# Two-layer hybrid backbone block: norm statistics, stage loads and context products in another program order

## The chip, the cores and the metric

The kernel runs on one core of one Trainium2 chip. The metric is the device time of one execution in microseconds (us); the kernel before has a median of 3649.86 us in 3 runs (3645.42 to 3652.5). TensorE (PE) multiplies, VectorE (DVE), ScalarE (ACT) and GpSimd (POOL) do elementwise work, and SyncE (SP) issues the DMAs.

## What is computed

Two layers over 1024 latent tokens and 256 context tokens, width 1024. In each layer a modulated RMS norm feeds one input projection, whose columns go to three mixers (neighbourhood attention, differential attention, a bidirectional SSD with a convolution over its `xbc` columns). Their outputs go through an output projection and a gated residual. A second modulated norm feeds a gated MLP with a convolution on its gate, again with a gated residual. The last layer needs no context output.

```python
h = rms_norm(x, g_mix[l]) * (1.0 + sc1) + sh1
hc = rms_norm(ctx, g_mix[l]) * (1.0 + csc1) + csh1
y, yc = token_mixers(h, hc, ...)
x = x + g1 * (y @ w_out[l])
h = rms_norm(x, g_ffn[l]) * (1.0 + sc2) + sh2
x = x + g2 * conv_glu(h, w_up[l], conv_w[l], conv_b[l], w_dn[l])
# if ctx_out: the same for ctx with c_ctx's modulation
```

## The kernel before

Activations lie transposed, 128 features by tokens, in three token chunks: 0 and 1 (512 tokens each) and 2 (the 256 context tokens). Float32 operands are split into a high and a low part by an ACT cast and a subtraction on DVE or POOL, and a product is three matmuls: high by high, high by low, low by high (`mm3`, L1214 to L1216; `proj_chunk`, L423 to L425).

The kernel is written in a tile framework: the order of the instructions on each engine, SP's among them, is planned when it is built. A list scheduler takes of the ready instructions the one that stands first in the program (`prio` shifts that) by modelled times. On the chip each engine then runs its list in that order. A tile waits for what lay in its memory before. Pools are stacks on the left or on the right of SBUF.

**The norm.** `norm_sq` squares on ACT and adds up on DVE (L376). `norm_scale` multiplies the sum by a matrix of ones (L382) and makes the reciprocal root on ACT and DVE (L411, L415). `norm_apply` scales (L397), modulates (ACT, L93), and splits into `h_0`, `h_1`, `h_2` for the three chunks (L402, L403). In the second norm `ffn_norm` is a generator whose first step is `norm_scale`; its rest makes the operands B11 to B22 and T1 to T4 of a Winograd-like scheme of seven products (L1592 to L1626).

**Output projection** (`outproj`). The last pass ends in chunk 1's norm sum. `up_prologue` then makes the first products of the up projection from chunk 0, and `up_weights` splits the first pair's weights (`T42` and `T43` are their slots); after that the norm generator is run to its end.

**Down projection** (`ffn_down`). `x1d` holds the residual stream, `hdd` the seven operands, `hcd` the context's. Layer 0 runs three groups of 3, 4 and 4 k-tiles, each with a context part (24 matmuls of 256 columns a step, with tiles `hc`) and seven products; layer 1 runs one group of 11 without context. `product` loops over the k-tiles: a `br` load from `hdd` (L1510, 2 buffers in layer 1, 3 in layer 0), `fetch(1)` of a weight tile `wd` (L1475, 18 buffers in layer 1, 10 in layer 0), casts and splits to `bH`, `bL`, `wH`, `wL` (L1220, L1223), and 12 matmuls into four PSUM banks A or B. The order is B11 (A), T2 (B), B21 (A), T3, T4 (B), T1, B22 (A). `w_s2` makes T2's weight on DVE in two steps (L1532, L1534). `to` evicts a bank into `xt` (L1438); the `xt` loads (`load_x`, L1481) stand in the program behind T2. In layer 0's last group the context norm for layer 1 (`norm_next(2)`) stands behind T2's evictions; its matmul takes a bank of tag B, and T2's four stay in use until T4 is done.

**Hand-over.** At the end of layer 0's down stage three weight tiles `w_pre` for layer 1's `xbc` columns are loaded and split. After the stage pool `dn0` is closed, `h1b` is opened on the right and `norm_apply` runs for chunk 1. Then `mixer(1)` opens `m1_1` on the left, with three `pad` tiles whose edges POOL sets to zero (L540). `proj_many` runs the products of `w_pre` in the order context, chunk 0, chunk 1, into three banks `mm`; ACT copies each result into `pad` (L548).

## Time and profile before

| | |
|---|---|
| median of 3 runs | 3649.86 us (3645.42 to 3652.5) |
| the profiled execution | 3640.75 us, span 3639.0 us |
| TensorE busy | 3292.2 us, 90% of the span, 17970 matmuls |
| DVE, ACT, POOL busy | 65%, 42%, 48% |
| mean granted TensorE clock | 0.962 of full speed |
| DMA | 491.24 MB, mean 135 GB/s |

All rows are of that one execution; times in a row are counted from the span's start. Layer 0's output projection ends at about 1060, its down stage runs from about 1664 to 1994, the hand-over lies at 1990 to 2060, layer 1's output projection ends at about 2890 and its down stage runs from about 3389 to the end. A granted clock of 1.00 is 2.4 GHz and 0.50 is 1.2 GHz. Busy time of overlapped matmuls is modelled, so PE's pace is read from the spacing of its instructions. A release in brackets is inferred from semaphore events.

### The profile page before, as it was taken

How to read it: one execution, taken by the hardware profiler on the slowest of the kernel's cores; microseconds unless marked ns; L12 is line 12 of the kernel's file. 1: busy time of each engine (PE TensorE's matmuls, PEld its weight loads, DVE VectorE, ACT ScalarE, POOL GpSimd, SP SyncE). 2: the span in 40 equal slices, each digit the busy share in tenths (PEclk: the TensorE clock that was granted, in tenths of full speed). 3: DMA queues.
4: the chain of work that ended last, by engine and by line, in shares of the span. 5: the costliest groups of instructions: out<-in, count | busy, mean ns of one | idle time of the engine just before them, and what ended most of it. 6: DMA issues, size and time to landing. Idle time of an engine off the chain costs nothing. (4 is left out here: it accounts for less than half of the span.)

```text
span 3639.0 us, 50284 instructions
## 1 busy us (share of the span) xinstructions
PE 3292.2 (90%) x17970; PEld 2590.3 (71%) x17970; DVE 2348.0 (65%) x4208; ACT 1514.2 (42%) x2641; POOL 1743.8 (48%) x1319
## 2 busy tenths in 40 slices
PE   7998898889998999998998798998888979999799
PEld 3876676666777887887787676776666757777587
DVE  6635875778376555556867554885784566667653
ACT  4232434677253333323335333344674533333243
POOL 2136563656233444444554126763664455555344
PEclk8999999999899999999999899998999989999899
DMA  8255444753721222226334136347555422222633
GB/s 292 99 198 164 128 128 133 187 152 102 254 93 67 87 93 68 87 92 213 118 117 138 46 127 208 124 131 184 168 150 198 156 70 91 101 96 88 225 107 119
DMA packets 328473, 491.24 MB, mean 135 GB/s; under 512 B 28320, under 2 KB 182048, under 8 KB 327968
## 3 DMA queue, kind: packets, MB, share of 16 engines
q1 hardware_dynamic: 328224, 488.03, 42.0%
q8 instruction: 142, 2.33, 0.3%
q14 instruction: 107, 0.88, 0.1%
HBM read 349.25 MB, written 138.67 MB: 134 GB/s over the span
## 5 line engine op out<-in xcount | busy, mean ns | idle before, releaser
L269 POOL TENSOR_TENSOR wL<-wr,wH 128x1024 fp32r<-128x1024 f32 x80 | 203.5, 2547 | 418.9 <-ACT wH L268 385.5
L1223 POOL TENSOR_TENSOR wL<-wr,wH 128x1024 fp32r<-128x1024 f32 (+1 forms) x102 | 211.1, 2072 | 336.5 <-ACT wH L1220 310.8
L1223 POOL TENSOR_TENSOR wL<-wd,wH 128x512 fp32r<-128x512 f32 (+1 forms) x134 | 211.3, 1594 | 229.7 <-ACT wH L1220 222.8
L1223 POOL TENSOR_TENSOR wL<-ws,wH 128x512 fp32r<-128x512 f32 x168 | 253.9, 1531 | 127.9 <-ACT wH L1220 127.7
L754 DVE TENSOR_SCALAR_CACHE_REDUCE e<-s 128x512 f32<-128x512 f32 (+1 forms) x400 | 228.3, 588 | 94.7 <-PE s L753 91.3
L1223 DVE TENSOR_TENSOR bL<-br,bH 128x512 fp32r<-128x512 f32 x154 | 146.4, 955 | 153.9 <-ACT bH L1220 153.5
L93 ACT ACTIVATE e<-e,nm 128x1280 f32<-128x1280 f32 (+1 forms) x144 | 183.0, 1271 | 55.9 <-DVE nm L757 52.5
L1220 ACT CAST wH<-ws 128x512 fp32r<-128x512 f32 x168 | 98.0, 619 | 236.5 <-PE mm L1215 111.2
L1220 ACT CAST wH<-wr 128x1024 fp32r<-128x1024 f32 (+1 forms) x102 | 91.7, 905 | 251.2 <-PE mm L1215 189.8
L753 PE MATMUL s<-ks,qst 128*128 128x512 f32 (+1 forms) x400 | 162.7, 443 | 36.6 <-DVE e L754 23.3
L772 POOL TENSOR_TENSOR e<-e 128x1280 f32<-128x1280 f32 (+1 forms) x72 | 192.6, 2675 | 3.9
L770 POOL TENSOR_SCALAR e<-e,rho 128x1280 f32<-128x1280 f32 (+1 forms) x72 | 89.3, 1240 | 188.8 <-DVE rho L762 80.2
L1369 DVE SCALAR_TENSOR_TENSOR fa<-fpad,vc,fa 128x1282 f32<-128x1282 f32 (+1 forms) x88 | 140.5, 1652 | 36.6 <-ACT fa L93 36.6
L992 POOL TENSOR_SCALAR mf<-cs,lah 128x128 fp32r<-128x128 f32 x288 | 139.8, 501 | 48.0 <-PE s L994 46.3
L1220 ACT CAST wH<-wd 128x512 fp32r<-128x512 f32 (+1 forms) x134 | 86.7, 683 | 166.4 <-PE B L1215 88.1
L423 PE MATMUL mm<-h_0H,wH 128*128 128x512 f32 x320 | 135.6, 425 | 21.2 <-ACT pad L548 15.1
L1220 ACT CAST bH<-br 128x512 fp32r<-128x512 f32 x154 | 95.5, 620 | 137.8 <-DMA br<-hdd 65.1
L1215 PE MATMUL A<-bL,wH 128*128 128x512 f32 x352 | 142.3, 404 | 7.3 <-DVE bL L1223 7.0
L1216 PE MATMUL A<-bH,wL 128*128 128x512 f32 x352 | 139.4, 400 | 0.0
L424 PE MATMUL mm<-h_0L,wH 128*128 128x512 f32 x320 | 131.9, 412 | 1.9 <-DVE h_0L L403 1.9
L423 PE MATMUL mm<-h_1H,wH 128*128 128x512 f32 x320 | 132.3, 414 | 1.5 <-ACT z L93 1.5
L753 PEld LDWEIGHTS s<-ks,qst 128*128 128x128 f32 x400 | 74.0, 198 | 81.5 <-DVE e L754 50.4
(871 smaller groups left out, 10835.8 us busy)
## 6 DMA issues: line engine op xcount, KB each, us to landing
wr<-in_w_up_dram SPq DMA_DIRECT2D x94, 512.0 KB
br<-hdd SPq DMA_DIRECT2D x154, 256.0 KB
wa<-in_w_ada_dram SPq DMA_DIRECT2D x56, 512.0 KB
wr<-in_w_in_dram SPq DMA_DIRECT2D x48, 512.0 KB
hdd<-c SPq DMA_DIRECT2D x88, 256.0 KB
wr<-in_w_ada_dram SPq DMA_DIRECT2D x40, 512.0 KB
wd<-in_w_dn_dram SPq DMA_DIRECT2D x38, 512.0 KB
hdd<-fa SPq DMA_DIRECT2D x66, 256.0 KB
```

What stands on the lines that cost most here:

```text
L93: ins = S.activation(**kw)
L269: (eng or G).tensor_tensor(out=wl, in0=wr, in1=wh.bitcast(F32), op=ALU.subtract)
L423: PE.matmul(ps[:, :n], wh[:, ks], r, start=(i == 0), stop=False)
L753: PE.matmul(s_, qst[b, qt][:, mi], ks[b][:, mi, k0 + c:k0 + c + n], start=True, stop=True)
L754: V.tensor_scalar(out=e[:, c:c + n], in0=s_, scalar1=1.0, scalar2=None, op0=ALU.mult, op1=ALU.max, accum_out=mx[:, ci:ci + 1])
L772: G.tensor_tensor(out=es[0][:, 0:nk], in0=es[0][:, 0:nk], in1=es[1][:, 0:nk], op=ALU.add)
L992: (V if hh % 2 else G).tensor_scalar(out=mf[:, hh], in0=C(mk), scalar1=lah[:, e, c, h:h + 1], scalar2=1.0, op0=ALU.mult, op1=ALU.mult)
L1215: PE.matmul(ps, wh, bl, start=False, stop=False, skip_group_check=True)
L1216: PE.matmul(ps, wl, bh, start=False, stop=last, skip_group_check=True)
L1220: S.copy(out=out_h, in_=src)
L1223: le.tensor_tensor(out=out_l, in0=src, in1=out_h.bitcast(F32), op=ALU.subtract)
L1369: V.scalar_tensor_tensor(out=a[:, :W], in0=pads[r][:, j:j + W], scalar=vcol(l, fw + j), in1=a[:, :W], op0=ALU.mult, op1=ALU.add)
```

## The change

Four things move in program order, and one pool moves in memory.

- In the down stage each weight tile and each `xt` tile is loaded by `fetch`, and each such load is tied behind the last operand load issued before it in the program (`lead`, a `br` or a context tile). It is an order on SP, without a semaphore. In layer 1 two such loads follow each `br`, the `xt` loads alternating with weights from the fifth weight on; in layer 0 two follow each context pair and three each `br`.
- In layer 0's last group the context norm for layer 1 stands ahead of B11, and chunk 0's `norm_scale` and half of chunk 1's squares ahead of B22.
- The context products of `w_pre` stand ahead of chunk 1's remaining squares and `norm_apply`; their copies into `pad` follow in the mixer.
- `m1_1` lies on the right instead of the left.
- In `outproj` the first step of the last norm generator (`norm_scale` of chunk 1) stands ahead of `up_prologue`.

```diff
-    def norm_apply(tmp, l, i, xt, ci, rs=None):
+    def norm_apply(tmp, l, i, xt, ci, rs=None, scaled=False):
...
-        scaled = rs is not None
-        if not scaled:
+        if rs is None:
             rs = norm_scale(tmp, ci)
...
-        with phase(f"m1_{l}") as p:
+        with phase(f"m1_{l}", "right" if l else "left") as p:
...
-            proj_many(w_pre, ALLC if l == 0 else [ALLC[2], ALLC[0], ALLC[1]], [xbc_ev(b) for b in range(nb)])
+            evs = [xbc_ev(b) for b in range(nb)]
+            for ev, ps in zip(evs, pre_ps):
+                with prio(-400):
+                    ev(ps, *ALLC[2])
+            proj_many(w_pre, MAINC if pre_ps else ALLC, evs)
+            pre_ps.clear()
...
+            lead = [None]
...
-                    todo = [(kt, h) for h in range(2) for kt in grp]
+                    pend = []
 
                     def fetch(n):
-                        for _ in range(min(n, len(todo))):
-                            kt, h = todo.pop(0)
+                        for _ in range(min(n, len(pend))):
+                            dst, src = pend.pop(0)()
+                            ins = SP.dma_start(out=dst, in_=src)
+                            if lead[0] is not None:
+                                tc.add_manual_dep(ins.ins, lead[0].ins.name, nosync, reason="order of loads")
+
+                    def load_raw_dn(kt, h):
+                        def go():
+                            raw[kt, h] = p.tile([128, 1024], F32, tag="wd", name="wd", bufs=10 if full else 18)
+                            return raw[kt, h], w_dn[l, (kt + h * NP) * 128:(kt + h * NP + 1) * 128, :]
+
+                        return go
+
+                    def load_xt(o, ci):
+                        c0, n = ALLC[ci]
+                        return lambda: (xt[o][:, c0:c0 + n], x1d[l][o, :, c0:c0 + n])
+
+                    xs = [load_xt(o, ci) for ci in ((2, 0, 1) if full else (0, 1)) for o in range(KT)] if gi == 0 else []
+                    for h in range(2):
+                        for kt in grp:
                             if pre_dn:
                                 raw[kt, h] = pre_dn.pop(0)
-                                continue
...
+                            else:
+                                pend.append(load_raw_dn(kt, h))
+                                if not full and len(pend) > 4 and xs:
+                                    pend.append(xs.pop(0))
+                    pend.extend(xs)
+                    fetch(2 if gi else 0)
...
-                    fetch(len(pre_dn) + 1)
...
+                    tail = fin and not last
+                    A = banks("A")
                     if full:
                         ps = banks("B")
...
-                                SP.dma_start(out=t.bitcast(F32), in_=hcd[l][kt + h * NP, e])
-                            fetch(1)
+                                lead[0] = SP.dma_start(out=t.bitcast(F32), in_=hcd[l][kt + h * NP, e])
+                            fetch(2)
...
-                        load_x(2)
...
+
+                    if tail:
+                        exp_tables()
+                        open_h(f"h{l + 1}")
+                        norm_next(2)
...
-                            SP.dma_start(out=br, in_=hdd[l][BN.index(nm), kt])
-                            fetch(1)
+                            lead[0] = SP.dma_start(out=br, in_=hdd[l][BN.index(nm), kt])
+                            fetch(3 if full else 2)
...
-                    load_x(0)
-                    load_x(1)
+                    fetch(len(pend))
                     to(A, [(1, 0), (1, 1), (0, 1)])
                     to(B, [(0, 1)])
-                    if tail:
-                        exp_tables()
-                        open_h(f"h{l + 1}")
-                        norm_next(2)
...
                     to(A, [(1, 1)], (1, 1))
+                    if tail:
+                        rs0 = norm_scale(tmp, 0)
+                        sq_next(1, range(4, 8))
                     product(A, "B22", w_s4, False, True)
                     if tail:
                         w_pre.extend(load_w(w_in[l + 1, B_XBC + b]) for b in range(3))
-                        sq_next(1, range(4, 8))
-                        norm_apply(tmp, l + 1, 0, xt, 0)
+                        norm_apply(tmp, l + 1, 0, xt, 0, rs0)
                     to(A, [(0, 1)], (0, 1))
             open_ps(mm=3)
             if not last:
+                c0, n = ALLC[2]
+                for wh, wl in w_pre:
+                    proj_chunk(wh, wl, c0, n, lambda ps, c0, n: pre_ps.append(ps))
                 open_h2(f"h{l + 1}b")
                 sq_next(1, range(0, 4))
                 norm_apply(tmp, l + 1, 0, xt, 1)
...
                 norms = [ffn_norm(l, tmp, xs[ci], ci, first) for ci in reversed(cis)]
+            next(norms[0])
             up_prologue(l, fx["n"])
```

## Rows read from the trace of the kernel before

**Rows 1.** The page, busy us (share of the span) x instructions of each engine.

```profile
PE 3292.2 (90%) x17970; PEld 2590.3 (71%) x17970; DVE 2348.0 (65%) x4208; ACT 1514.2 (42%) x2641; POOL 1743.8 (48%) x1319
```

**Rows 2.** Windows, layer 1's down stage: busy by engine, PEclk, DMA share, GB/s.

```profile
3420.00:3430.00 10.00, 4.24 (x10) 3.38 (x11) 4.79 (x8) 0.62 (x1) 0.00 (x0) 0.50 1.05 404
...
3470.00:3480.00 10.00, 10.00 (x46) 8.29 (x45) 4.46 (x4) 4.06 (x7) 4.28 (x3) 1.00 0.31 90
```

**Rows 3.** SP in time, both down stages: start, us issuing, line, what, count.

```profile
1677.78 2.79 SPq L1475 DMA_DIRECT2D wd<-in_w_dn_dram  x4
...
3401.14 0.33 SPq L1510 DMA_DIRECT2D br<-hdd  x1
3402.40 8.45 SPq L1475 DMA_DIRECT2D wd<-in_w_dn_dram  x9
...
3419.32 0.32 SPq L1510 DMA_DIRECT2D br<-hdd  x1
```

**Rows 4.** ACT in time, layer 1's down stage; brackets: idle before, its end.

```profile
3409.34 0.62 ACT L1220 CAST bH<-br 128x512 fp32r<-128x512 f32 x1 [5.07 <-DMA br<-hdd]
...
3425.09 0.62 ACT L1220 CAST bH<-br 128x512 fp32r<-128x512 f32 x1 [9.48 <-DMA br<-hdd]
```

**Rows 5.** PE in time, hand-over from layer 0's down stage to layer 1's mixer.

```profile
2003.83 0.28 PE L425 MATMUL mm<-h_2H,wL 128*128 128x256 f32 x1
...
2008.23 2.07 PE L382 MATMUL t<-acc,cs 128*128 128x512 f32 x2 [4.12 <-DVE acc L376]
...
2025.45 0.80 PE L423 MATMUL mm<-h_0H,wH 128*128 128x512 f32 x1 [15.14 <-ACT pad L548]
...
2045.16 0.40 PE L423 MATMUL mm<-h_1H,wH 128*128 128x512 f32 x1
```

**Rows 6.** POOL and DVE in time, the same hand-over.

```profile
2023.12 0.17 POOL L540 MEMSET pad<- 128x2 f32 x3 [1.69 <-DVE h_1L L403]
...
2023.60 2.50 DVE L403 TENSOR_TENSOR h_1L<-xt,h_1H 128x512 fp32r<-128x512 f32 x4 [0.53 <-ACT h_1H L402]
```

**Rows 7.** DVE and PE in time, end of layer 0's output projection.

```profile
1059.08 0.69 DVE L376 TENSOR_TENSOR acc<-acc,sq 128x512 f32<-128x512 f32 x1 [0.76 <-ACT sq L93]
...
1069.61 1.02 PE L382 MATMUL t<-acc,cs 128*128 128x512 f32 x2
...
1104.08 0.79 PE L1214 MATMUL mm<-T30H,wH 128*128 128x512 f32 x1 [3.77 <-DVE u L1329]
```

**Rows 8.** POOL and PE in time, end of layer 1's output projection.

```profile
2911.61 16.94 POOL L1223 TENSOR_TENSOR wL<-T42H,wH 128x512 fp32r<-128x512 f32 x1 [9.42 <-ACT wH L1220]
...
2928.61 0.80 PE L1216 MATMUL mm<-T10H,wL 128*128 128x512 f32 x1 [14.47 <-POOL wL L1223]
```

**Rows 9.** The chain that ended last: start us, us, what (layer 1's T2 products).

```profile
3465.16 0.91 PE B L1214 x4
...
3467.88 0.91 PE B L1214 x4
```

**Rows 10.** PE in time, waits in the down stages of both layers.

```profile
1682.57 1.19 PE L1214 MATMUL B<-hcH,wH 128*128 128x256 f32 x4 [6.46 <-DMA hcH<-hcd]
...
1919.08 0.80 PE L1215 MATMUL B<-bL,wH 128*128 128x512 f32 x1 [4.53 <-DVE bL L1223]
...
1973.52 0.72 PE L1215 MATMUL A<-bL,wH 128*128 128x512 f32 x1 [2.76 <-DVE bL L1223]
...
3393.12 1.73 PE L1214 MATMUL A<-bH,wH 128*128 128x512 f32 x4 [4.30 <-ACT bH L1220]
```

**Rows 11.** DVE in time, first eviction of B in layer 1's down stage.

```profile
3482.88 0.75 DVE L1438 SCALAR_TENSOR_TENSOR xt<-B,mods,xt 128x512 f32<-128x512 f32 x1 [1.53 <-PE B L1216]
```

**Rows 12.** Tiles xt and wd: line, operation, count, ns min/median/max, starts, forms.

```profile
L1438 DVE SCALAR_TENSOR_TENSOR xt<-A,mods,xt x96: 733/740/751, 1705.3 to 3635.2; 128x512 f32<-128x512 f32 x96
...
L1534 DVE TENSOR_TENSOR s<-wd x16: 683/692/2859, 1677.2 to 3423.7; 128x512 f32<-128x512 f32 x16
...
L1223 POOL TENSOR_TENSOR wL<-wd,wH x134: 1260/1302/2854, 1669.4 to 3621.9; 128x512 fp32r<-128x512 f32 x114, 128x1024 fp32r<-128x1024 f32 x20
```

More of the change, by code (lines that the diff above doesn't have):

```diff
@@ L1228, in hybrid_kernel @@
     pre_dn = []
+    pre_ps = []
     pre_wd = []
@@ L1471, in fetch @@
+                    xs = [load_xt(o, ci) for ci in ((2, 0, 1) if full else (0, 1)) for o in range(KT)] if gi == 0 else []
+                    for h in range(2):
+                        for kt in grp:
                             if pre_dn:
                                 raw[kt, h] = pre_dn.pop(0)
-                                continue
-                            raw[kt, h] = p.tile([128, 1024], F32, tag="wd", name="wd", bufs=10 if full else 18)
-                            SP.dma_start(out=raw[kt, h], in_=w_dn[l, (kt + h * NP) * 128:(kt + h * NP + 1) * 128, :])
@@ L1477, in load_x @@
-                    def load_x(ci):
-                        if gi == 0:
-                            c0, n = ALLC[ci]
-                            for o in range(KT):
-                                SP.dma_start(out=xt[o][:, c0:c0 + n], in_=x1d[l][o, :, c0:c0 + n])
-                    fetch(len(pre_dn) + 1)
+                            else:
+                                pend.append(load_raw_dn(kt, h))
+                                if not full and len(pend) > 4 and xs:
+                                    pend.append(xs.pop(0))
@@ L1545, in w_s4 @@
                         return t
-                    tail = fin and not last
-                    A = banks("A")
                     product(A, "B11", lambda kt: quarter(0, 0, kt), True, False)
@@ L1715, in hybrid_kernel @@
                     SP.dma_start(out=x0[k][:, c0:c0 + n], in_=xin[:, k, c0:c0 + n])
-        norm_apply(tmp, 0, 0, x0, 0, rs)
+        norm_apply(tmp, 0, 0, x0, 0, rs, True)
         for ci in range(1, 3):
```

## The prediction, made before the changed kernel was run

> **What bounds the kernel now.** I read the page first: TensorE is busy 90% of the span [rows 1], so only stretches in which it waits, or runs at the lower clock, can give time back. I then took 10 us windows over the places that the diff touches, and in them PE's timeline with what ended each idle gap. Three places lose much.
>
> First, the start of layer 1's down stage. Two windows show the contrast: PE busy 4.24 of 10 us at a granted clock of 0.50 (the 1.2 GHz level) with the DMA engines full at 404 GB/s, and later 10.00 of 10 us at clock 1.00 with 90 GB/s [rows 2]. SP's queue shows why: between the `br` issued at 3401.14 and the next one at 3419.32 stand nine `wd` weight loads (8.45 us of issuing, 0.94 each), then `xt` loads [rows 3]; the late `br` is cast only at 3425.09 [rows 4]. The bulk loads have free buffers from the start, `br` has two, so the planner let all bulk loads pass.
>
> Second, the hand-over from layer 0's down stage to layer 1's mixer: TensorE waits 4.12 us for the norm sum, then 15.14 us for the ACT copy into `pad` [rows 5]. That copy waits for `pad`'s memsets, and these for `h_1L` [rows 6]: on the left, `pad` lies where `xt` lay, and `xt` is read until the last norm step.
>
> Third, layer 0's output projection ends in a norm chain for which TensorE waits 3.77 us at its end [rows 7], and layer 1's in a wait of 14.47 us [rows 8].
>
> **Part 1, loads tied to their order (layer 1's down stage).** No work is added; the 18 `wd` and 16 `xt` loads go out two behind each `br`, instead of ahead. One step (12 matmuls) takes 2.72 us when nothing is missing [rows 9]. B11 and T2 have 11 steps each, 22 x 2.72 = 59.8 us; from the first product at 3393.12 [rows 10] to the first eviction of B at 3482.88 [rows 11] it is 89.8 us. The excess, 30.0 us, is the most that can come back. What is late next: (a) the two first steps move 0.26 + 1.05 MB, the loaded ones after them 0.26 + 0.79 MB; at 404 GB/s [rows 2] that is 3.2 and 2.6 us against 2.72: about 2 us lag in all. (b) DVE in T2: two weight differences and a low split, 3 x 0.69 [rows 12], 2.1 us in each step, and 12 evictions of A at 0.74 [rows 12], 8.9 us, before B21 may start: 31.7 us of DVE in 29.9. Before, the differences ran inside the stall. Group 2 of layer 0 has the same crowding in four steps, and TensorE waited 4.53 us there for `bL` [rows 10]. Eleven steps could cost 2.75 times that, 12.5 us, or the bare 2 us; I take 6, near the one stall that a row shows. Sum: 30.0 - 2 - 6 = **22 us saved**, ends 15 and 28. On SP, a `br` that waits for its buffer now holds back the loads queued behind it, but each of these is used four or more steps later (the `wd` of step 4 goes out behind the `br` of step 0), and that distance, 10.9 us, covers it.
>
> **Part 2, `pad` on the right, context products ahead of the second half's statistics.** `pad` and `cacc` (3 x 5152 + 2 x 5136 bytes, 25.1 KB per partition) now lie below `h1b` (32 KB), and both below `h1`. The stage pool `dn0` (66 KB by its buffers) ended under `h1` already, so the 57.1 KB below `h1` fall into `dn0`'s stretch and not into `xt`'s. `dn0`'s tiles are free when B22 ends, before any context product. Those were the first chunk before, too; they end at 2004.1 [rows 5]. Then come L382 (1.0 us at the higher clock [rows 7]) and 72 products on `h_0` at 2.72 / 12 us, 16.3 us: 2021.4. `h_1` was complete 15.8 us after the end of L382 (2010.30 to 2026.10 [rows 5, 6]), so now at 2020.9, in time. The first `h_1` product comes at 2021.4 instead of 2045.16 [rows 5], 23.8 us. This needs `h_0` by 2005; its statistics now run ahead of B22, and DVE is rid of the context norm there. GpSimd has three weight splits to do in the same stretch; a split held up by a DVE run took 16.94 us once [rows 8], and half of that in front of a context product would leave 15, the whole of it 7. I take **19 us**, ends 8 and 26 (the upper one if the 2.76 us wait in T1 and B22 [rows 10] goes too).
>
> **Part 3, layer 0's context norm ahead of B11 (group 2).** Nothing is added, and no DMA moves. 16 DVE steps of 256 columns, some 0.35 us each as half of a 512-column one [rows 12], 5.6 us, and as many on ACT move from the T1 and B22 products to B11 and T2, where DVE is already late by 4.53 us [rows 10]. T2's fourth PSUM bank waits for this norm's matmul, which B11's 10.9 us cover; without that cover it costs the norm's sum, within the same 8 us. Price 0 to 8, taken 4; given back in T1 and B22 0 to 2.76 [rows 10], taken 2. **2 us lost.**
>
> **Part 4, layer 0's group 0.** The weights of the next group, four of them issued at 1677.78 [rows 3], no longer go in front of the `hc` tile that TensorE waited 6.46 us for [rows 10]. But three early `br` now bring nine `xt`, 2.4 MB, 5.8 us at 404 GB/s, to the same place. **2 us saved**, ends -2 and 6.
>
> **Part 5, statistics ahead of the early products.** Layer 0: the last sum is done at 1059.77, its matmul ran at 1069.61 behind products, and TensorE's last wait for the chain ends at 1104.08 [rows 7]. Earlier by 9.8 us at best, 9 with the matmul's own time. But layer 1 shows what a DVE run without a gap does to GpSimd: a split that takes 1.30 us [rows 12] took 16.94 us, and TensorE waited 14.47 us for it [rows 8]. In layer 0 the splits of pair 0's weights lie next to the run, and moved forward the run meets the last of them, with TensorE's context rows behind. Between -4 and 9 us, **3 us saved**. Layer 1: the same held-up split ends the wait, so **nothing**, 0 to 3. The Trainium skill (SBUF — State Buffer, Who interferes with whom) says that a DVE instruction with two SBUF inputs and a GpSimd one that reads SBUF exclude each other for the whole of one instruction; by that rule alone a split would wait 0.7 us and layer 0 would give the 9 us. The row disagrees in size: 16.94 us is the run, not one instruction.
>
> **The sum.** 22 + 19 - 2 + 2 + 3 = 44 us. The profiled execution took 3640.75 us (span 3639.0), so 3597 by it; the median of the three runs, 3649.86, lies 9.1 us above, which gives **3606 us**. Between these places every stretch is shifted, not changed.
>
> **The rivals.**
> (A) DVE's earlier runs hold up GpSimd: layer 0's output projection loses 4 us instead of winning 3, part 2 gives 8, part 3 loses 8. For it: [rows 8]. Against: the median split takes 1.30 us beside DVE [rows 12]. 3606 + 7 + 11 + 6 = 3630 us.
> (B) The tied loads pace the stage: the loop of two `br` runs at 3.6 us for each of 17 loaded steps. 17 x 3.6 + 5 x 2.72 + 6 = 80.8 us, 9 saved instead of 22: 3619 us.
> (C) The change doesn't do what it says: `pad` still waits, or the planner puts the products where they were. Part 2 gives nothing: 3625 us. For it: the order of instructions is planned by modelled times, which no view shows.
> (D) Slower: in the loop of (B), `br` lands behind its tied loads each time. From 3401.14 to its cast at 3409.34 it took 8.2 us [rows 3, 4]; with three issues of 0.94 and 1.3 us of splits, 12.3 us for two steps, 6.15 for one. 17 x 6.15 + 5 x 2.72 + 6 = 124 us against 89.8: part 1 loses 34 and the whole is 3662 us. It decides from 5.5 us a step on. Against: at that pace the DMA engines would idle more than half of the time, and `br` would land sooner.
> (E) The new plan costs elsewhere what is won here: 3649 us.
>
> **How the numbers follow.** Forecast 50%, A 18%, B 11%, C 9%, D 5%, E 7%. The forecast's own range is 3586 to 3620, by the ends of parts 1 and 2 that can come together. With A, B and C the range is 3586 to 3634; D, E and part of the tails lie outside. A measurement of this kernel can tell 0.2%, 7 us. Faster by more: forecast, A, B, C, 88%; within it: E, 7%; slower: D, 5%.
>
> **What would show it.** Right: one `br` and two bulk loads alternate on SP after 3389 or its like; the granted clock stays at 1.00 from there; B's first eviction comes some 22 us sooner after the first A product; no idle time of TensorE is ended by `pad`; `h_1` products stand directly behind those on `h_0`. Wrong: GpSimd splits over 5 us in new places (A); products that wait for `bH` in every step (B, D); waits for `pad` (C); another length from the hand-over to layer 1's output projection (E).

## The result, and the profile after

The changed kernel took 3589.18 us (median of 4 runs, 3588.71 to 3605.27) against 3648.49 us (3645.42 to 3652.5, 4 runs) for the kernel before beside it: a ratio of 0.9848, 95% interval 0.9818 to 0.9877. It is 1.5% faster, inside the predicted range and 17 us below the predicted 3606. Its profiled execution has a span of 3587.6 us (3589.41 us in all), 51.4 us less than the span before.

The page has the engines' busy time, as [rows 1] did. The four engines have the same numbers of instructions, PE's share rises from 90% to 92%:

```profile
PE 3284.6 (92%) x17970; PEld 2582.9 (72%) x17970; DVE 2350.0 (66%) x4208; ACT 1515.8 (42%) x2641; POOL 1766.9 (49%) x1319
```

Layer 1's down stage, windows of 10 us (columns as in [rows 2]): the stretch at clock 0.50 with PE busy 4.24 is gone. The worst window now has 7.42 and a clock of 0.66, DMA still full; the later one is as in [rows 2].

```profile
3360.00:3370.00 10.00, 7.42 (x20) 5.63 (x20) 6.71 (x9) 3.22 (x6) 3.63 (x3) 0.66 1.03 378
3370.00:3380.00 10.00, 9.65 (x42) 7.96 (x43) 7.15 (x8) 3.30 (x6) 5.39 (x4) 1.00 1.04 412
...
3440.00:3450.00 10.00, 10.00 (x46) 8.29 (x45) 7.30 (x9) 4.15 (x7) 4.87 (x5) 1.00 0.36 102
```

SP's queue there, in time, answers to [rows 3]: one `br`, one `wd`, one `xt` in turn. In [rows 3] nine `wd` and six `xt` loads stood between two `br`.

```profile
3371.17 0.32 SPq L1535 DMA_DIRECT2D br<-hdd  x1
3371.53 0.43 SPq L1477 DMA_DIRECT2D wd<-in_w_dn_dram  x1
3372.01 0.43 SPq L1477 DMA_DIRECT2D xt<-x1d  x1
3373.57 0.32 SPq L1535 DMA_DIRECT2D br<-hdd  x1
```

The row of 8.45 us in [rows 3] is not issuing time, and my 0.94 us for one load was a wrong reading: the row merges nine issues and the gaps between them. Each took 0.33 us, and their starts lie 0.61 to 1.25 us apart; two of the nine, kernel before:

```profile
3404.89 0.33 SPq L1475 DMA_DIRECT2D wd<-in_w_dn_dram  x1
...
3406.14 0.33 SPq L1475 DMA_DIRECT2D wd<-in_w_dn_dram  x1
```

What SP waited for in the gaps no run shows. That the `br` stood behind the bulk loads does not hang on it.

The hand-over, PE in time, answers to [rows 5]: the waits of 4.12 and 15.14 us are gone but for 1.06 us at the norm's sum, `h_0` follows the sum at once, and `h_1` stands behind 17.2 us of products on `h_0`.

```profile
1996.94 1.13 PE L382 MATMUL t<-acc,cs 128*128 128x512 f32 x2 [1.06 <-DVE acc L376]
1997.51 0.80 PE L422 MATMUL mm<-h_0H,wH 128*128 128x512 f32 x1
...
2014.70 0.40 PE L422 MATMUL mm<-h_1H,wH 128*128 128x512 f32 x1
```

The end of the two output projections, POOL and PE in time, answers to [rows 7, 8]. In layer 0 there is now what only layer 1 had: one GpSimd split, of 1024 columns, lasts 20.61 us, and TensorE waits 17.41 us for it. Layer 1 has its wait of 14.47 us as before.

```profile
1075.07 20.61 POOL L1227 TENSOR_TENSOR wL<-wr,wH 128x1024 fp32r<-128x1024 f32 x1 [8.36 <-ACT wH L1224]
1095.73 0.58 PE L1220 MATMUL s<-c0H,wL 128*128 128x256 f32 x1 [17.41 <-POOL wL L1227]
1106.15 0.50 PE L1218 MATMUL mm<-T30H,wH 128*128 128x512 f32 x1 [0.78 <-DVE u L1334]
...
2875.97 16.94 POOL L1227 TENSOR_TENSOR wL<-T42H,wH 128x512 fp32r<-128x512 f32 x1 [9.42 <-ACT wH L1224]
2892.96 0.79 PE L1220 MATMUL mm<-T10H,wL 128*128 128x512 f32 x1 [14.47 <-POOL wL L1227]
```

To account for every microsecond I cut each span at the same events, read off PE's and DVE's timelines, and compare the pieces (us). No edit of the change stands in I, III, VI and VIII, though in VI the planned order came out different.

- I: start to the first norm sum (L382) of layer 0's output projection
- II: from there to the second set of T3 products of layer 0's up stage (norm, early products, first pair)
- III: to the last T3 of that stage
- IV: layer 0's down stage, to the first product on `h_2`
- V: the hand-over, to the first product of layer 1's dt weights
- VI: layer 1's mixer, to the first norm sum of its output projection
- VII: to the first T3 of layer 1's up stage
- VIII: to its last T3
- IX: to the first eviction of B in layer 1's down stage (B11 and T2)

From there to the end it is 156 us in all kernels.

| kernel | I | II | III | IV | V | VI | VII | VIII | IX |
|---|---|---|---|---|---|---|---|---|---|
| before | 1016.0 | 108.6 | 529.0 | 340.2 | 132.7 | 724.0 | 87.1 | 441.4 | 103.9 |
| changed | 1013.3 | 111.0 | 523.8 | 339.1 | 108.8 | 718.8 | 87.1 | 444.9 | 84.7 |
| changed, again | 1019.0 | 111.2 | 524.1 | 339.0 | 108.8 | 723.0 | 87.1 | 444.2 | 85.1 |
| statistics behind products | 1017.7 | 108.5 | 529.4 | 338.1 | 109.0 | 728.7 | 87.1 | 442.8 | 85.6 |
| pads left | 1016.2 | 110.9 | 527.1 | 339.2 | 126.7 | 727.0 | 87.1 | 443.6 | 85.6 |
| loads untied | 1015.2 | 110.4 | 526.8 | 341.8 | 108.8 | 728.8 | 87.1 | 444.8 | 106.3 |
| context norm late | 1015.1 | 111.2 | 526.7 | 337.9 | 121.1 | 735.1 | 87.6 | 441.9 | 85.5 |
| tied loads alone | 1014.4 | 107.8 | 530.1 | 329.8 | 134.6 | 721.2 | 87.1 | 443.4 | 86.4 |
| pair 0 on DVE | 1014.7 | 102.7 | 525.0 | 335.5 | 109.0 | 724.9 | 84.2 | 445.3 | 85.5 |
| the same, statistics behind | 1016.9 | 107.0 | 526.9 | 340.2 | 108.8 | 716.1 | 84.2 | 443.4 | 83.8 |
| fewer tied | 1016.9 | 111.3 | 526.5 | 336.7 | 108.8 | 716.1 | 87.1 | 443.4 | 88.0 |
| difference in B11 | 1022.4 | 111.4 | 524.0 | 338.7 | 108.8 | 719.9 | 87.1 | 444.1 | 86.2 |
| evictions spread | 1015.8 | 111.0 | 523.4 | 339.2 | 109.0 | 729.2 | 87.1 | 444.8 | 83.8 |
| pair 0 and evictions | 1012.1 | 102.6 | 526.0 | 341.5 | 108.8 | 735.9 | 84.7 | 443.2 | 84.1 |

Of the 51.4 us, 23.9 are in V, 19.2 in IX and 1.1 in IV; II gave 2.4 back. That makes 41.8 us where the edits are. The other 9.6 us are in I, III, VI and VIII. In the second execution of the same program (next section) the edited pieces give 41.3 us, and these four together are as long as before, within 0.2 us.

### The profile page after: what moved, and what is told of

Its sections match the earlier page's. It is cut to its first block, busy times and chain, and to the rows that moved or that the text cites. A ratio compares the mean times of both kernels' runs of the same rounds, so it can differ in the third digit from the quotient of the medians.

```text
span 3587.6 us, 50299 instructions
## 1 busy us (share of the span) xinstructions
PE 3284.6 (92%) x17970; PEld 2582.9 (72%) x17970; DVE 2350.0 (66%) x4208; ACT 1515.8 (42%) x2641; POOL 1766.9 (49%) x1319
## 5 line engine op out<-in xcount | busy, mean ns | idle before, releaser
L1227 POOL TENSOR_TENSOR wL<-wr,wH 128x1024 fp32r<-128x1024 f32 (+1 forms) x102 | 228.6, 2243 | 339.0 <-ACT wH L1224 304.4
L1219 PE MATMUL A<-bL,wH 128*128 128x512 f32 x352 | 141.7, 403 | 11.9 <-DVE bL L1227 11.7
```

Source lines behind the costliest of these rows:

```text
L1219: PE.matmul(ps, wh, bl, start=False, stop=False, skip_group_check=True)
L1227: le.tensor_tensor(out=out_l, in0=src, in1=out_h.bitcast(F32), op=ALU.subtract)
```

## The experiments

**The changed kernel once more.** How much of a difference between two profiles is the edit, and how much is any second execution?

> The changed kernel once more, unaltered, beside the other three on this chip. If the stretches that no edit touches (from the start to layer 0's output projection, 1013.3 us; from layer 1's first dt product to its output projection, 763.1 us; the two up stages, 523.8 and 444.9 us) differ between two executions of one program, they should move by up to 5 us here; if their lengths belong to the planned program, they should come back within 1 us and the differences of 5 to 10 us seen in the four kernels with one part undone are a new plan's. Total 3585 to 3600 us.

It took 3596.41 us, 0.986 of the kernel before beside it (0.9828 to 0.9892). Its profiled span is 3597.5 us, 9.9 us more than the first one's, from the same program: +5.6 in I, +4.2 in VI, and at most 0.8 in any other piece. II, IV, V, VII and IX agree within 0.4 us. So the 9.6 us that the first comparison has in untouched pieces are no effect of the change that I could show; the totals of one kernel scatter by 10 us and more (3585.35 to 3599.53 here). From here on I judge the pieces, and the totals only where they differ by more than that.

How far a piece can be trusted shows in the runs below that leave the order of PE's matmuls in it as in the changed kernel: II lies within 1.0 us there (110.4 to 111.4), V within 0.2 and VII at 87.1, but IX within 2.6 (83.8 to 86.4) and IV within 4.7 (335.5 to 340.2). In III all fourteen executions have one order on PE and take 523.4 to 530.1 us; nearly all of that lies in one of its twenty intervals, which takes 24.4 to 31.0 us.

**Each part undone.** Loads without the tie:

```
-  if lead[0] is not None:
+  if False:
       tc.add_manual_dep(ins.ins, lead[0].ins.name, nosync, reason="order of loads")
```

> The changed kernel without the ties between the loads: the list of loads and its alternation stay, only the order on SP is free. Theory (the tie is what counts, since the bulk loads have free buffers and pass the operand loads): in layer 1's down stage the operand loads stand behind bulk loads again, the time from the first A product to the first eviction of B goes from 73 to 85 to 92 us, layer 0's group 0 loses 2 to 6 us, total 3602 to 3612. Rival (the position in the program, residual tiles alternating with weights, does it): within 4 us of 73 us, total 3587 to 3593.

3626.49 us, 0.9958 (0.9943 to 0.9973). SP in time, and 10 us windows at the start of layer 1's stage:

```profile
3384.90 0.32 SPq L1535 DMA_DIRECT2D br<-hdd  x1
...
3395.68 0.32 SPq L1535 DMA_DIRECT2D br<-hdd  x1
...
3395.00:3405.00 10.00, 4.72 (x12) 3.23 (x11) 8.16 (x12) 1.75 (x3) 3.31 (x2) 0.67 1.04 414
3405.00:3415.00 10.00, 3.76 (x9) 2.42 (x8) 6.63 (x10) 0.00 (x0) 0.00 (x0) 0.67 1.04 409
```

Between the two `br` there are 11 bulk loads, and the two windows are the picture of [rows 2]. IX is 106.3 us, 21.2 to 21.7 more than with the tie and 2.5 more than before. IX is longer than before perhaps because the new list also has `xt` loads early; B11 and T2 alone take 95.1 us where 85 to 92 was expected, and the total came out above the expected 3602 to 3612, VI and III being longer too. The theory holds: the order on SP is the stall.

`pad` on the left:

```
-  with phase(f"m1_{l}", "right" if l else "left") as p:
+  with phase(f"m1_{l}") as p:
```

> The changed kernel with the mixer's first pool on the left again; program order as in the changed kernel. Theory (the place of the pad tiles makes the hand-over's gain): the copies into pad wait for the last norm step, TensorE idles some 15 to 20 us between the context products and those on chunk 0, the first product on chunk 1 comes 17 to 24 us later than at 2014.7, total 3606 to 3613. Rival (the earlier statistics and the new place of the context products make it): the wait is under 6 us and the total under 3596.

3621.0 us, 0.9946 (0.9927 to 0.9965). PE in time, the hand-over:

```profile
2003.34 1.13 PE L382 MATMUL t<-acc,cs 128*128 128x512 f32 x2 [1.21 <-DVE acc L376]
2019.61 0.79 PE L422 MATMUL mm<-h_0H,wH 128*128 128x512 f32 x1 [15.14 <-ACT pad L547]
```

The wait of [rows 5] is back to the hundredth, and V is 17.9 us longer. The total is above the expected 3606 to 3613, since III and VI are longer too. The place of the context products was not undone by itself.

The context norm behind T2 again, where it was (the four lines of `if tail:` with `norm_next(2)` moved back):

> The changed kernel with layer 0's context norm behind T2's evictions again, where its matmul waits for a bank until T4 is done. Theory (part 3 only shifts DVE work between two crowded places): the waits for the low split at T2 and B21 of group 2 fall from 7.8 to about 4.5 us, those in T1 and B22 rise by 0 to 4, total within 3 us of the changed kernel, 3586 to 3592. Rival (the early context norm is what frees DVE for chunk 0's norm at the hand-over): the first product on chunk 0 comes 5 to 12 us later, total 3594 to 3601.

3612.32 us, 0.9923 (0.9905 to 0.9941). PE in time, the hand-over:

```profile
2002.78 0.50 PE L422 MATMUL mm<-h_0H,wH 128*128 128x512 f32 x1 [2.40 <-ACT pad L547]
2017.25 1.02 PE L382 MATMUL t<-acc,cs 128*128 128x512 f32 x2
2025.62 1.65 PE L422 MATMUL mm<-h_1H,wH 128*128 128x512 f32 x3 [3.63 <-ACT h_1H L401]
```

V is 12.3 us longer: the norm sum comes 14.5 us behind the `h_0` product shown, where it stood ahead of them all before, and `h_1` is late by 3.63 us. The waits shown and some smaller ones are 7.5 us together; behind them the granted clock is 0.50 and 0.54 in the windows 2025 to 2030 and 2030 to 2035, where the changed kernel keeps 1.00, and the 72 products on `h_1` take 21.8 us and not 16.8. So the free place of `pad` gives its full gain only with the early context norm, and my theory, that this part only shifts DVE's work and leaves the total within 3 us, fell. The rival foresaw a loss at the hand-over, but in another place: it had `h_0` late. The cost in the down stage can be seen too: from the first B11 product of group 2 to the first product on `h_2`, PE's timeline has 95.6 us here and 102.7 and 102.2 us in the two executions of the changed kernel. The early context norm costs 7 us (5 to 8 over all kernels with it) and brings 12.

The statistics behind the early products again (`next(norms[0])` left out):

> The changed kernel without part 5: the first step of the last norm generator stands behind the early products again, as before; the rest of the change stays. In the changed kernel TensorE waited 17.41 us in layer 0's output projection for GpSimd's low split of the pair's second weight tile. Theory (GpSimd is held up by DVE's run, which part 5 put ahead of the split): that wait goes, the six waits of before (3.8 us and less) come back, the first T3 product of layer 0 comes at 1104 instead of 1106 and the total is that of the changed kernel within 2 us, 3587 to 3591. Rival (the earlier statistics shorten the chain as forecast and the 17.41 us wait only took the place of the others): 3 to 9 us slower, 3592 to 3598. Layer 1's wait of 14.47 us stays by both.

3603.28 us, 0.9888 (0.9869 to 0.9907). POOL and PE in time, layer 0:

```profile
1076.10 2.61 POOL L1227 TENSOR_TENSOR wL<-wr,wH 128x1024 fp32r<-128x1024 f32 x1 [6.60 <-ACT wH L1224]
...
1078.76 0.39 PE L1220 MATMUL s<-c0H,wL 128*128 128x256 f32 x1 [2.18 <-POOL wL L1227]
...
1105.80 0.80 PE L1218 MATMUL mm<-T30H,wH 128*128 128x512 f32 x1 [3.44 <-DVE u L1334]
```

The split takes 2.61 us, and II is 2.5 us shorter than in the changed kernel, as in the kernel before. By its own piece the part loses 2.5 us. The total says the opposite, but the 14 us by which it is above the first run of the changed kernel lie in I, III and VI, and VI has another planned order here.

**One part alone.** The kernel before with the tied loads and nothing else of the change.

> The kernel before with the loads tied to their order and nothing else of the change. Theory (the parts are independent, and the ties are worth what their removal cost): layer 1 from the first A product to B's first eviction 72 to 76 us instead of 89.8, the hand-over unchanged at 130 to 134 us with its wait for pad, total 18 to 26 us below the kernel before. Rival (without the earlier context norm and the free pad the ties move loads into other stages): under 12 us.

3618.73 us, 0.9933 (0.9911 to 0.9955), 24 us less than before: IX saves 17.4, IV 10.4, V loses 1.9. In IX the tie alone is worth somewhat less than its removal cost; the other parts were not run alone. The 10.4 us in IV are not settled: the kernel with the late context norm has the same order on PE there and takes 337.9 us, 8 more, of which 6.8 are in group 0's context products (27.1 and 20.3 us). PE in time, the hand-over, has both old waits:

```profile
1999.30 2.07 PE L382 MATMUL t<-acc,cs 128*128 128x512 f32 x2 [8.58 <-DVE acc L376]
2016.51 0.80 PE L422 MATMUL mm<-h_0H,wH 128*128 128x512 f32 x1 [15.14 <-ACT pad L547]
```

**Who holds up whom in the norm.** The changed kernel with pair 0's low parts made by DVE where they met its run (`ld` is DVE for pair 0, `le` for pair 0 of layer 1):

```
-  split2(*d, r2, S, G)
+  split2(*d, r2, S, ld)
-  split2(c[0][:, 0:512], c[1][:, 0:512], s1, S, G)
+  split2(c[0][:, 0:512], c[1][:, 0:512], s1, S, le)
...
```

> Pair 0's low weight parts that meet the norm's DVE run are made by DVE and not by GpSimd: the 1024 columns of the last weight in layer 0, all of pair 0's in layer 1. Theory (GpSimd's split is held up for as long as DVE runs without a gap, and TensorE waits for the split): the waits of 17.41 us (layer 0) and 14.47 us (layer 1) for the low weight part go; layer 0 from its first output-projection row of the norm to the second T3 product comes down from 111.0 to 104 to 108 us, layer 1 from its first norm row to the first T3 product from 42.8 to 30 to 36 us; 10 to 18 us less in all than the changed kernel on this chip. Rival (DVE's own chain sets the end, and now has 2 to 4 us more to do): each stretch changes by less than 3 us, a wait for a DVE result of about the same length takes the place, and the total is within 5 us of the changed kernel.

3590.89 us, 0.9856 (0.9826 to 0.9887). PE in time, both layers:

```profile
1096.79 0.79 PE L1218 MATMUL mm<-T30H,wH 128*128 128x512 f32 x1 [3.60 <-DVE u L1334]
...
2882.25 0.50 PE L1219 MATMUL mm<-T13L,wH 128*128 128x512 f32 x1 [1.86 <-DVE T13L L1227]
2886.47 0.80 PE L1219 MATMUL mm<-T20L,wH 128*128 128x512 f32 x1 [3.48 <-DVE T20L L1227]
2891.89 0.50 PE L1219 MATMUL mm<-T23L,wH 128*128 128x512 f32 x1 [1.08 <-DVE T23L L1227]
2896.10 0.80 PE L1218 MATMUL mm<-T30H,wH 128*128 128x512 f32 x1 [3.48 <-DVE u L1334]
```

Both long waits are gone. Layer 0 follows the theory: II falls from 111.2 to 102.7 us. Layer 1 follows the rival: it gains 2.9 us (counted from the second norm sum 42.8 to 40.0, in VII 87.1 to 84.2) and not 7 to 13. In place of two waits, 14.47 us for the split and 2.27 us for the last `u`, there are seven of 0.3 to 3.5 us from 2876 on, 11.9 us together, six for DVE's own results and one for ACT's: the run of DVE that held up GpSimd was the chain itself. In layer 0 the held-up split stood ahead of the context rows and of the T1 products, and DVE's results were long done.

To see what the early statistics are worth once nothing waits for GpSimd, the same with `next(norms[0])` left out:

> Pair 0's low parts on DVE as in the run where they took layer 0's norm stretch from 111.2 to 102.7 us, but with the statistics behind the early products again, as before the change. Theory (the early statistics are worth up to 9 us in layer 0, and only the held-up GpSimd split ate it): layer 0's stretch comes back to 107 to 112 us, so the early statistics are worth 5 to 9 us once no split waits for DVE; layer 1's stretch stays within 2 us of 84.2 (84.21 with the statistics ahead), since its chain was DVE's run either way. Rival (the split was the whole cost, and the early statistics are worth nothing): layer 0's stretch stays at 102 to 104 us.

3587.46 us, 0.9865 (0.9837 to 0.9893). II is 107.0 us, so the early statistics are worth 4.3 us with the split on DVE, just under the 5 to 9 that I had given them, and cost 2.5 us with it on GpSimd. VII is the same 84.2 us: in layer 1 they are worth nothing. PE in time, layer 0: the wait for the split is short, and the wait for the last `u` is the one of [rows 7].

```profile
1076.87 0.38 PE L1220 MATMUL s<-c0H,wL 128*128 128x256 f32 x1 [1.12 <-DVE wL L1227]
...
1103.96 0.50 PE L1218 MATMUL mm<-T30H,wH 128*128 128x512 f32 x1 [3.45 <-DVE u L1334]
```

**What is left at the start of layer 1's down stage.** Of the 73.2 us from the first A product to the first eviction of B, 13.3 are more than the 59.8 of bare steps. First the loads, one behind each `br` in B11 and the weights ahead of `xt`:

```
-  if not full and len(pend) > 4 and xs:
+  if False:
...
-  fetch(3 if full else 2)
+  fetch(3 if full else 1 if nm == "B11" else 2)
```

> Layer 1's down stage ties one bulk load behind each br in B11 (two in T2, as before), the weights first and then xt. Theory (what is left of the stall at the start of the stage is DMA volume: 1.31 MB for a step of 2.72 us keeps the DMA engines full for the first 30 us): from the first A product to B's first eviction 64 to 69 us instead of 73.2, the first two steps under 4 us each and not 6, DMA share under 0.9 there. Rival (two br buffers and the chain br, ACT, DVE set the first steps, at a granted clock of 0.66 or less): 72 to 76 us, with the DMA engines less busy.

3593.45 us, 0.9868 (0.9842 to 0.9894). The piece got longer, 76.7 us instead of 73.2 and 73.9, so the expectation failed, and for a reason that neither side had. B11 itself did get shorter: 34.9 us to the first B product instead of 39.4 and 37.3 (the second step 3.3 us instead of 5.4 and 5.5, the first 6.5 as before). But T2 lost more. DVE, POOL and PE in time, T2:

```profile
3395.41 1.78 DVE L1559 TENSOR_TENSOR s<-wd 128x512 f32<-128x512 f32 x1
...
3398.50 1.78 DVE L1559 TENSOR_TENSOR s<-wd 128x512 f32<-128x512 f32 x1
...
3404.94 0.68 DVE L1559 TENSOR_TENSOR s<-wd 128x512 f32<-128x512 f32 x1
...
3391.64 5.00 POOL L1227 TENSOR_TENSOR wL<-s,wH 128x512 fp32r<-128x512 f32 x3 [3.44 <-ACT wH L1224]
3397.91 1.82 POOL L1227 TENSOR_TENSOR wL<-s,wH 128x512 fp32r<-128x512 f32 x1 [1.27 <-ACT wH L1224]
3401.32 3.15 POOL L1227 TENSOR_TENSOR wL<-s,wH 128x512 fp32r<-128x512 f32 x2 [1.59 <-ACT wH L1224]
...
3405.07 0.64 PE L1219 MATMUL B<-bL,wH 128*128 128x512 f32 x1 [3.38 <-DVE bL L1227]
```

A weight difference on DVE takes 1.78 us beside a split on GpSimd and 0.68 us at 3404.94, when GpSimd is idle. The low part `bL` stands behind these differences. That this is the whole loss is not shown.

Next, T2's first weight difference made in B11 (`w_s2`'s subtraction moved into B11's weight function):

> The first of T2's two weight differences is made in B11, from the same raw weights, in both layers; the work is the same. Theory (DVE in T2 is the crowded engine: two differences, one low split and twelve evictions): layer 1 from the first A product to B's first eviction 68 to 70 us instead of 73.2, and in layer 0's group 2 most of the waits of 4.11, 1.42 and 2.25 us in T2 go, in the three groups together 5 to 10 us; total 7 to 14 us less than the changed kernel on this chip. Rival (T2's waits come from br's late landing or from GpSimd, which DVE's work holds up wherever it stands): both stretches within 2 us of the changed kernel, the waits move to B11.

3592.37 us, 0.9862 (0.9837 to 0.9887). Nothing moved: IX 86.2 us, and PE's waits in T2 of group 2 and at B21's start are 4.09, 1.42 and 2.25 us where the changed kernel has 4.11, 1.42 and 2.25. The edit asked for what the planner had done already. In the changed kernel DVE's timeline has this difference (L1557) early in B11, while T1's (L1564) stand from 3380 on, five of them in T2, though T1 starts only at 3523:

```profile
3361.83 0.68 DVE L1557 TENSOR_TENSOR wd<-wd 128x512 f32<-128x512 f32 x1
...
3392.77 0.69 DVE L1564 TENSOR_TENSOR wd<-s,wd 128x512 f32<-128x512 f32 x1
...
3395.40 1.59 DVE L1564 TENSOR_TENSOR wd<-s,wd 128x512 f32<-128x512 f32 x1
3396.92 2.71 DVE L1443 SCALAR_TENSOR_TENSOR xt<-A,mods,xt 128x512 f32<-128x512 f32 x4
3399.55 0.68 DVE L1227 TENSOR_TENSOR bL<-br,bH 128x512 fp32r<-128x512 f32 x1
```

So the run was no test of DVE's load, but these rows show what stands ahead of `bL`: evictions of A. In group 2 of layer 0 (DVE, POOL and PE in time, changed kernel) all twelve do:

```profile
1900.16 7.99 DVE L1443 SCALAR_TENSOR_TENSOR xt<-A,mods,xt 128x512 f32<-128x512 f32 x12
...
1901.16 2.56 POOL L1227 TENSOR_TENSOR wL<-wd,wH 128x512 fp32r<-128x512 f32 x2 [4.14 <-ACT wH L1224]
...
1908.06 0.68 DVE L1227 TENSOR_TENSOR bL<-br,bH 128x512 fp32r<-128x512 f32 x1
...
1908.80 0.50 PE L1219 MATMUL B<-bL,wH 128*128 128x512 f32 x1 [4.11 <-DVE bL L1227]
```

The POOL row tells something of the held-up splits above: these two took 1.30 and 1.29 us inside a run of twelve evictions without a gap. An eviction has one input in PSUM and one in SBUF; the run that held up GpSimd subtracts and adds, with both inputs in SBUF. So a run of DVE without a gap is not enough; whether it is the inputs or the operation, which differs too, these rows do not tell.

The evictions of A's banks tied behind later low parts of T2:

```
   ins = acc(j + 4 * r, ci, ps[j])
+  if behind:
+      i = min((j + 1) * len(grp) // 4, len(grp) - 1) if full else 2 * j + 2
+      tc.add_manual_dep(ins.ins, lows[behind, i].ins.name, nosync, reason="evict later")
```

> In T2 of both layers' down stages the evictions of A's four banks are each tied behind a later low part bL of T2 (in groups of 3 and 4 steps behind those of steps 0 or 1 to the last, in layer 1 behind those of steps 2, 4, 6 and 8) and no longer stand in one run of 4 to 12 in front of the second step's bL. No work is added. Theory (T2's stalls are the planned order on DVE, evictions ahead of the next bL): the waits of T2 in layer 0's group 2, 4.11, 1.42 and 2.25 us, come down to 4 us or less together, the whole layer 0 down stage from 325.7 us to 315 to 322, layer 1's stretch from the first A product to B's first eviction from 73 to 69 to 71. Rival (DVE has more work in T2 than T2 is long, in whatever order): B21 then waits for the evictions of A as long as T2 waited for bL, and each stretch stays within 2 us.

3599.63 us, 0.9888 (0.9862 to 0.9914). DVE and PE in time, group 2 of layer 0:

```profile
1912.82 4.03 DVE L1443 SCALAR_TENSOR_TENSOR xt<-A,mods,xt 128x512 f32<-128x512 f32 x6
...
1916.90 0.49 PE L1218 MATMUL A<-bH,wH 128*128 128x512 f32 x1 [1.47 <-DVE xt L1443]
1925.09 0.79 PE L1219 MATMUL A<-bL,wH 128*128 128x512 f32 x1 [7.69 <-DVE bL L1227]
```

In layer 0 the rival holds: T2 has no wait left, and B21 waits 9.2 us, where the changed kernel waits 7.8 in the two together. That fits the rival's reason, that with three or four steps DVE has more to do there than TensorE, in whatever order. In layer 1, where T2 has eleven steps, IX is 83.8 us, which a kernel without this edit has too (pair 0 on DVE, statistics behind), so no gain is shown.

Both edits together, pair 0 on DVE and the evictions spread:

> The evictions spread and pair 0's low parts on DVE, together on the changed kernel. If the two savings are independent, layer 0's norm stretch is 102 to 104 us, layer 1's 39 to 41 us, and the two down stages are as in the run with the evictions alone; 12 to 25 us less than the changed kernel, so 3565 to 3582 us on a chip where that takes 3590. Rival: the evictions gain nothing, and it is as pair 0 alone, 3578 to 3588.

3595.44 us, 0.9867 (0.9842 to 0.9892): II 102.6, VII 84.7, IX 84.1, each about as with its edit alone, but IV 341.5 and VI 735.9, so that the total is no better. VI's order on PE is that of the changed kernel in four other executions (again; pair 0 with the statistics behind; fewer tied; difference in B11), which with it take 716.1 to 723.0 us. The other eight kernels with an edit have other orders there, 721.2 to 735.9 us, and the two longest, this one and the one with the late context norm, share one. So an edit ahead can change VI's plan and its length, but need not.

Pair 0 on DVE is 11.4 us shorter than the changed kernel in the pieces that it edits (II and VII), and its median on the same chip was 5.5 us lower, inside the scatter. No kernel here is shown to beat the changed one in total.

## Why the prediction was right, and where it was off

| step | forecast | measured |
|---|---|---|
| Part 1, first A product to B's first eviction | 22 saved (15 to 28) | 15.9 to 16.6; with the time before it, all of IX, 18.8 to 19.2 (21.2 to 21.7 by removal, 17.4 alone) |
| Part 2, hand-over | 19 saved (8 to 26) | 23.9 in V |
| Part 3, context norm early | 2 lost | 7 lost by removal (5 to 8) |
| Part 4, layer 0's group 0 | 2 saved | between -1 and 6, not settled |
| Part 5, layer 0 / layer 1 | 3 saved / 0 | 2.4 to 2.5 lost / 0 |
| profile to median | 9.1 us added | 0 for the changed kernel |

**Part 1** held in mechanism; its size came out near the lower end. In the stretch that I had summed, 89.8 us became 73.2 and 73.9. IX starts 2.6 us better, at the last T3, and that was in no term. The mis-sized term is the lag of the start: I gave it 2 us, and T2 6 us of crowding. On PE's timeline the first steps of B11 took 6.1, 5.1, 5.7, 15.8 and 7.1 us before; now they take 6.6, 5.4, 2.9, 2.7 and 2.7. So the stall behind the bulk loads is gone, but the two first steps, 12.0 us against 5.4 of bare ones, stayed as long as they had been. I had worked them out from volume alone; in the first window the granted clock is 0.66, and the DMA engines have a share of 0.96 to 1.04 for 30 us. Altogether B11 takes 37.3 to 39.4 us against 29.9 of bare steps, 7 to 10 us more, and T2 about 4 to 7 (33.5 us before, 33.8 and 36.6 now). In T2 I named the right engine for the wrong reason: not two differences in every step, one is done in B11, but evictions and differences that nobody needs yet, planned ahead of `bL`. The 0.94 us for one issue, in the first paragraph and in rival D, is the wrong reading of [rows 3] named above; the sum of part 1 does not use it.

**Part 2** came out at the 23.8 us that I had worked out, not at the 19 that I took. The 5 us I kept back were for a GpSimd split held up in front of a context product; between 1997 and 2014 PE has no wait at all. The condition that the step named, `h_0` by 2005, is not the one that decided: 2005 is 11.2 us behind the first product on `h_2`, and even with the late context norm the first product on `h_0` comes 9.3 us behind it. What the late norm delays is chunk 1's sum, 26.7 us behind that product instead of 10.0, and with it `h_1`; 12.3 of the 23.9 us go by that. The step had `h_1` in time, and named DVE being rid of the context norm only for `h_0`.

**Part 3** was mis-sized. Price 4, of which 2 given back: measured 7, and nothing given back, the waits in T1 and B22 are still 0.67, 1.83 and 3.00 us, against 2.76 [rows 10], 1.02 and 0.52. My upper bound of 8 was the right end. In IV it does not show. With the ties and the late norm IV is 2.3 and 10.4 us shorter than before, in two kernels of one order, so the ties may save there what the early norm costs; how much, the scatter of IV leaves open.

**Part 4.** The context products of group 0 took 25.9 us before and 20.7 in the changed kernel, but 20.0 to 27.1 among kernels that have the same ties. It is open what of this is the edit.

**Part 5** failed in layer 0 as rival A described it: the run moved forward met the last split. The failed step is the weighing: I set the 9 us of gain against a stall that I had read in layer 1 and took 3. That stall was the likelier outcome by the rows that I quoted: moved forward by 9 us, DVE's run has no gap from 1063 to 1093, the split comes at 1075, and [rows 8] says that it then waits for the run's end. Of rival A's other terms, part 2's did not come, and part 3's did in size alone (7 of 8 us): TensorE's waits in group 2 are for DVE's `bL`, not for GpSimd. Rivals B, C and D did not come about: no step of the tied stage takes 3.6 us throughout (from the third on most of B11's take 2.7 to 2.9), no wait for `pad` is left, and the changed kernel's `br` are not behind their loads. Of E one thing is true: layer 1's mixer comes out in several planned orders and varies by up to 20 us, which can hide or feign what a part is worth.

By pieces the forecast sum of 44 us stands against 41.8 measured. The 17 us between 3606 and 3589 come from elsewhere: 9.6 us are in the untouched pieces, where the second execution of the same program has no gain at all, and 9.1 us are the step from the profiled execution to the median. On four more occasions the kernel before had medians of 3642.2 to 3644.6 us; the 3649.86 that I scaled to was high, and the profiled 3640.75 about 2 to 4 us low. The second run of the changed kernel, 3596.4, is 10 us from the forecast.

The Trainium skill (SBUF — State Buffer, Who interferes with whom) has two rules that bear on this. That a DVE instruction with two SBUF inputs contends with a GpSimd instruction that reads SBUF: the trace agrees in both directions, 0.68 to 1.78 us for a DVE difference beside a split, 2.61 to 20.61 us for a split beside DVE's run. That whoever issues first gets the shared pair for the whole instruction and the other is blocked: DVE's loss of 1.1 us fits it, but GpSimd's is the rest of the run, 18 us over some thirty DVE instructions, and not the 0.7 us of one instruction that I had made of the rule in part 5.

## What to carry to other kernels

Look at the queue that issues loads before asking for bandwidth: one small load stood behind fifteen large ones, and an order tie that adds no work gave back 16 to 22 us. When a chain on one engine is moved forward, list what other engines have in the same microseconds, and take the stall that a row shows as the forecast and not as the tail; here 2.5 us lost became 4.3 us won once the one split was moved to the engine that held it up. And cut two profiles at the same events before a part is judged by totals: in two executions of one program the pieces that mattered agreed to 0.4 us where the spans differed by 10. Over more runs some pieces scatter by 3 to 5 us, so a gain of that size needs more than one run.

## What was not expected of the hardware

A GpSimd subtraction of 1024 columns lasted 20.61 us beside a gapless run of DVE and ended 2.2 us after the last of its instructions, against 2.60 to 2.61 us in the same place in the three kernels where the run comes later. It did so in all eight executions that have it there, to 0.02 us. Beside a run of evictions, with one input in PSUM, splits kept their 1.3 us. The other way about DVE lost 1.1 us for one split and went on. Two executions of one program differ by 5.6 us in the first 1016 us alone, 4.1 of it between 360 and 400 us. And SP's issues of bulk loads lay 0.61 to 1.25 us apart in the untied queue, each 0.33 us long, where tied pairs follow each other within 0.5 us.
